# A softmax kernel whose first six loads are issued from two queues in place of one

## The chip, the core and the metric

The kernel runs on one core of one Trainium2 chip. The metric is the device time of one execution in microseconds (us), the median of several.

Four engines of the core matter. SP (SyncE) only issues transfers. ACT (ScalarE) computes the exponentials and issues the stores. DVE (VectorE) computes maxima, reciprocals and divisions. The transfers themselves are carried out by 16 DMA engines. A queue is the list in which the transfers of one issuing engine stand; in the profile SP's is q1 and ACT's is q10.

## The reference

A softmax with a temperature over the last axis of a 32 x 512 x 1024 array of float32, that is over 16,384 rows of 1024 numbers:

```
scaled = x / temperature                      # temperature 0.5
shifted = scaled - max(scaled, axis=-1)
exp_x = exp(shifted)
out = exp_x / sum(exp_x, axis=-1)
```

64 MB (67.11 million bytes) are read and as many are written, each once.

## The kernel before

The rows are cut into 16 tiles of 4 MB: 128 partitions, each with 8 whole rows (32,768 contiguous bytes). Six buffers hold tiles. A tile is loaded, worked on in place in two groups of four rows per partition, and stored; when its store is issued, the load that reuses its buffer is put into SP's queue, where it waits for that store to land.

```python
TILES = [[8]] * 16
BUFS = 6
GROUP = 4
    ...
    def load():
        i = len(tiles)
        if i < len(TILES):
            xt = data.tile([P, sum(TILES[i]), d], f32, name="xt")
            nc.sync.dma_start(out=xt, in_=dram(xf, i))          # SP's queue
            tiles.append(xt)

    def maximum(g):          # VectorE: one reduction over 128 x 4096, then the bias
        ...
    def exponential(g):      # ScalarE: 4 x exp over 128 x 1024, row sums on the way
        ...
    def divide(g):           # VectorE
        ...
        nc.vector.reciprocal(recip, sums)
        for b in range(k):
            nc.vector.tensor_scalar_mul(
                tiles[i][:, a + b, :], in0=tiles[i][:, a + b, :], scalar1=recip[:, b : b + 1]
            )

    def store(g):            # once per tile
        ...
            nc.scalar.dma_start(out=dram(of, i)[:, a : a + k, :], in_=tiles[i][:, a : a + k, :])
            ...
                load()

    with tc.manual_schedule():
        for _ in range(BUFS):
            load()
        for g in range(len(groups) + 1):
            if g < len(groups):
                maximum(g)
                exponential(g)
            if g > 0:
                divide(g - 1)
                store(g - 1)
```

## Time and profile before

| | before |
|---|---|
| time, median of 3 | 317.91 us (317.78 to 318.01) |
| bytes moved | 134.25 MB |
| VectorE busy | 235.5 us of a span of 316.0 |
| ScalarE busy | 149.6 us |
| first load landed | 12.6 us |
| VectorE starts | 13.0 us |
| last store issued | 302.4 us |

These are lines of the profile's page of the kernel before. The busy line gives microseconds and share of the span. In the DMA line each digit is the busy share of the 16 DMA engines in one fortieth of the span, in tenths, where 9 means 90% or more. The q lines give packets, MB, and the share of 16 engines' time. The next lines give the chain of waits that ended last, by engine, and the group of reductions (busy us, mean ns, then VectorE's idle time just before them and what ended it). The last two give issue to landing in us.

```profile
span 316.0 us, 620 instructions
DVE 235.5 (75%) x224; ACT 149.6 (47%) x257; POOL 0.2 (0%) x4
DMA  8999999999999999999999999999999999999996
q1 hardware_dynamic: 2304, 67.11, 49.7%
q10 hardware_dynamic: 2304, 67.11, 49.2%
q14 instruction: 4, 0.03, 0.0%
DVE 49%; DMA 32%; another core or an unknown queue 9%; ACT 5%; issue 1%; DVEq 0%; SPq 0%
L70 DVE TENSOR_REDUCE top<-xt 128x4 f32<-128x4096 f32 x32 | 141.3, 4416 | 62.6 <-DMA xt<-in_x_dram 62.6
xt<-in_x_dram SPq DMA_DIRECT2D x16, 4096.0 KB, 50.2
out_dram<-xt ACTq DMA_DIRECT2D x16, 4096.0 KB, 38.6
```

The DMA line is the one to read first: after the first slice it is 9 in every slice but the last. The two queues together hold 98.9% of the 16 engines' span. The line of the chain, which puts VectorE first with 49%, says something else and must be doubted: a chain walks back through whatever released each instruction, and it can pass through an engine whose slowness held nobody up.

The columns are from and to (us), length, busy time of VectorE, ScalarE and POOL with the number of instructions, clock, busy share of the DMA engines, and GB/s:

```profile
4.00:32.00 28.00, 18.69 (x16) 12.63 (x20) 0.00 (x0) 1.00 1.00 433
32.00:38.00 6.00, 5.93 (x6) 3.25 (x7) 0.00 (x0) 1.00 0.94 350
76.00:260.00 184.00, 140.84 (x135) 90.30 (x157) 0.00 (x0) 1.00 1.00 433
260.00:300.00 40.00, 30.03 (x30) 19.19 (x34) 0.00 (x0) 1.00 1.01 434
```

Only loads move from 4 to 32 us, loads and stores from 76 to 260. The rate is 433 GB/s in both. The one exception inside is the stretch from 32 to 38 us. The packet records of the trace show more of it than this view, because each packet of 32,768 bytes has its own start and duration there: nearly all take 1.213 us, but 16 at the start and 27 between 32 and 36 us take more, 1.3 to 2.6 us.

### The profile page before, as it was taken

The numbers are of one execution on the slowest core, as the hardware profiler recorded it, in microseconds if no ns is written. First come the engines' busy times: TensorE is split into PE (matmuls) and PEld (weight loads), VectorE is DVE, ScalarE is ACT, GpSimd is POOL, SyncE is SP. The second block draws the span as 40 slices with busy tenths as digits, with TensorE's granted clock in tenths as the row PEclk, the third lists the DMA queues.
The fourth block names the chain that finished last, engine by engine and source line by source line (L and its number), as shares of the span: only waits on it lengthen the run. The fifth ranks groups of instructions, "written<-read, shape, count | busy, mean of one in ns | idle before, by whom it ended". The sixth has DMA issues, their size and how long they took to land.

```text
span 316.0 us, 620 instructions
## 1 busy us (share of the span) xinstructions
DVE 235.5 (75%) x224; ACT 149.6 (47%) x257; POOL 0.2 (0%) x4
## 2 busy tenths in 40 slices
DVE  0399999999689494994949859497693976949720
ACT  0176666666526255361554605546064560645500
POOL 0000000000000000000000000000000000000000
DMA  8999999999999999999999999999999999999996
GB/s 332 411 452 423 373 460 415 452 425 431 436 427 440 427 444 423 444 419 448 415 452 411 452 408 456 423 444 427 436 431 432 440 423 444 419 444 419 452 411 274
DMA packets 4612, 134.25 MB, mean 425 GB/s; under 512 B 512, under 2 KB 512, under 8 KB 512
## 3 DMA queue, kind: packets, MB, share of 16 engines
q1 hardware_dynamic: 2304, 67.11, 49.7%
q10 hardware_dynamic: 2304, 67.11, 49.2%
q14 instruction: 4, 0.03, 0.0%
HBM read 67.11 MB, written 67.11 MB: 425 GB/s over the span
## 4 chain that ended last, share of the span: by engine, by line
DVE 49%; DMA 32%; another core or an unknown queue 9%; ACT 5%; issue 1%; DVEq 0%; SPq 0%
DVE top L70 29%; DMA xt<-in_x_dram 20%; DVE xt L93 18%; DMA out_dram<-xt 12%; ACT xt L79 5%; DVE recip L91 1%; DVE bias L73 1%; DVEq L147 0%; SPq L61 0%
## 5 line engine op out<-in xcount | busy, mean ns | idle before, releaser
L79 ACT ACTIVATE xt<-xt,bias 128x1024 f32<-128x1024 f32 x128 | 145.4, 1137 | 136.8 <-DVE recip L91 119.4
L70 DVE TENSOR_REDUCE top<-xt 128x4 f32<-128x4096 f32 x32 | 141.3, 4416 | 62.6 <-DMA xt<-in_x_dram 62.6
L93 DVE TENSOR_SCALAR xt<-xt,recip 128x1024 f32<-128x1024 f32 x128 | 87.7, 749 | 1.1
L79 ACT ACTIVATION_READ_ACCUMULATOR xt<-xt,bias 128x1 f32 x128 | 23.9, 187 | 0.0
L79 ACT ACT_TABLE_LOAD x1 | 1.3, 1283 | 13.0 <-DMA xt<-in_x_dram 13.0
L91 DVE RECIPROCAL recip<-sums 128x4 f32<-128x4 f32 x32 | 5.5, 171 | 2.1 <-ACT xt L79 2.1
L73 DVE TENSOR_SCALAR bias<-top 128x4 f32<-128x4 f32 x32 | 5.4, 170 | 1.1
L133 POOL MEMSET const-bfloat16-1.0<- 128x1 bf16 x1 | 0.1, 101 | 0.0
L133 POOL MEMSET const-uint8-127<- 128x1 uint8 x1 | 0.1, 101 | 0.0
L133 POOL MEMSET const-float32-0.0<- 128x1 f32 x1 | 0.1, 98 | 0.2 <-issue 0.2
L133 POOL MEMSET const-float32-1.0<- 128x1 f32 x1 | 0.1, 98 | 0.0
## 6 DMA issues: line engine op xcount, KB each, us to landing
xt<-in_x_dram SPq DMA_DIRECT2D x16, 4096.0 KB, 50.2
out_dram<-xt ACTq DMA_DIRECT2D x16, 4096.0 KB, 38.6
```

What stands on the lines that cost most here:

```text
L70: nc.vector.tensor_reduce(out=top, in_=tiles[i][:, a : a + k, :], axis=mybir.AxisListType.X, op=extreme)
L73: nc.vector.tensor_scalar_mul(bias, in0=top, scalar1=-scale)
L79: nc.scalar.activation(tiles[i][:, a + b, :], tiles[i][:, a + b, :], mybir.ActivationFunctionType.Exp, bias=bias[:, b : b + 1], scale=scal ...
L91: nc.vector.reciprocal(recip, sums)
L93: nc.vector.tensor_scalar_mul(tiles[i][:, a + b, :], in0=tiles[i][:, a + b, :], scalar1=recip[:, b : b + 1])
L133: nc = _bacc.Bacc("TRN2", target_bir_lowering=False, num_devices=1)
```

## The change

The intent is to fill the buffers sooner: ACT has nothing to do at the start, so it issues every second one of the six first loads. The later ten loads stay with SP.

```diff
         if i < len(TILES):
             xt = data.tile([P, sum(TILES[i]), d], f32, name="xt")
-            nc.sync.dma_start(out=xt, in_=dram(xf, i))
+
+            queue = nc.scalar if i < BUFS and i % 2 else nc.sync
+            queue.dma_start(out=xt, in_=dram(xf, i))
             tiles.append(xt)
```

## The prediction

> **What bounds the kernel now: the 16 DMA engines.** The page counts 134.25 MB; by the packet records of the trace 4096 packets of 32,768 bytes carry almost all of it. A packet takes 1.213 us, from either queue, in either direction: 256 per engine are 310.5 us, and 16 engines give 432 GB/s. The records have 16 packets in flight in every microsecond from 2 to 312: loads only (before 34 us), mixed, and stores only (after 282 us), all at 433 GB/s. First packet 1.74, last end 314.8. VectorE is busy 235.5 us and ScalarE 149.6 of 316.0 (page, busy times); their waits (VectorE 62.6 us for loads) are slack. The chain of waits names VectorE for 49%, which misleads: no DMA engine was starved by it.
>
> The only loss inside is slow packets: 16 at the start (one per engine, about 0.7 us over 1.213) and 22 at 34 to 37 us, just after the first store was issued on ACT's so far unused queue (median 1.66 us; about 0.8 us of bandwidth).
>
> **What the change does.** SP issues loads 0, 2, 4; ACT loads 1, 3, 5. Three issues leave SP (0.33 to 0.53 us each; all six end by 3.6 us), three of about 0.34 us come to ACT, which is idle until 13 us anyway. None is on the critical path: SP's first issue already fills the engines from 2 us on. The Trainium skill, "DMA: Bandwidth & Descriptors", section "Issuing engines are not separate DMA queues", says that DMAs of different issuers run on the same 16 engines and interleave, and that several issuers save only issuing time. This trace agrees: 433 GB/s with one queue active and with two.
>
> What moves:
> - Loads 0 and 1 share the engines packet by packet. Loads landed at 12.6, 22.3, 32.0 us; now in pairs, near 22, 41 and 61. VectorE starts near 22 instead of 13.0 us.
> - ACT's queue is first in, first out: store 0, issued near 42 us (32.7 before), stands behind load 5, starts near 60.5 and lands near 70.5 (57.1 before); load 6 is issued near 71 (57.6).
> - From 60 to 71 only stores move, then both at half rate each. The last load lands near 266 (282.1), the last store is issued near 286 (302.4); about five queued stores end the run.
>
> Engines stay full: when loads stop, stores 0 and 1 are ready. VectorE's 9 us later start is paid from its 80 us of idle time. The 310.5 us are unchanged.
>
> Only slow packets can change. If those at 34 us belong to the first use of ACT's queue, they now coincide with the start: up to 0.8 us gained. If they belong to a queue joining, they recur when SP's queue restarts near 72 us: nothing gained.
>
> **Prediction: 317.4 us** (before 317.91), eight in ten between 316.7 and 318.5. Faster by over 2%: 0.01; within 2%: 0.96; slower: 0.03.
>
> **What would show it.** Right: DMA at 9 or full in every slice, about 425 GB/s; VectorE's first wait about 22 us, the sum of its waits unchanged; longer landing of stores; last load about 16 us earlier. Wrong: fewer than 16 packets in flight near 60 to 75 us or at the end, or many packets over 1.3 us.
>
> **What would make it wrong.** A slow spell at every restart of SP's queue (ten loads, about 0.8 us each: up to 8 us slower), if that queue runs empty between loads; ACT blocked at issuing because its queue holds too much (SP's held six without blocking); uneven sharing of the engines, which would shift landings but not the sum.

## The result and the profile after

The changed kernel took 318.06 us (median of 6, 317.86 to 318.14), the kernel before 318.01 us (median of 6, 317.78 to 318.39). The ratio is 1.000, with a 95% interval from 0.9987 to 1.0012: the same. Here and below, a ratio with an interval is the mean time of one kernel's fast runs over that of the other's of the same rounds, so it is not quite the ratio of the medians that stand beside it.

The lines of the page after that answer to those above:

```profile
span 316.3 us, 619 instructions
DVE 235.1 (74%) x224; ACT 149.6 (47%) x257; POOL 0.2 (0%) x4
DMA  8999999999999999999999999999999999999995
q10 hardware_dynamic: 2736, 79.69, 58.6%
q1 hardware_dynamic: 1872, 54.53, 40.2%
q14 instruction: 5, 0.04, 0.0%
DMA 54%; DVE 32%; ACT 5%; issue 1%; DVEq 0%; SPq 0%
L72 DVE TENSOR_REDUCE top<-xt 128x4 f32<-128x4096 f32 x32 | 141.3, 4416 | 50.5 <-DMA xt<-in_x_dram 50.5
out_dram<-xt ACTq DMA_DIRECT2D x16, 4096.0 KB, 45.7
xt<-in_x_dram SPq DMA_DIRECT2D x13, 4096.0 KB, 27.0
xt<-in_x_dram ACTq DMA_DIRECT2D x3, 4096.0 KB, 41.0
```

Work moved between queues (three loads, 12.58 MB, went from q1 to q10), landing times moved, and the chain of waits now puts the DMA engines first with 54% in place of 32%. The DMA line did not move, and nor did the time. The chain's shares changed by 20 points in a kernel that takes as long as before; that is how little they say here.

In stretches:

```profile
4.00:32.00 28.00, 9.20 (x5) 6.07 (x10) 0.00 (x0) 1.00 1.00 432
32.00:38.00 6.00, 5.96 (x6) 4.38 (x8) 0.00 (x0) 1.00 1.01 437
56.00:62.00 6.00, 5.93 (x6) 3.24 (x7) 0.00 (x0) 1.00 0.97 355
76.00:260.00 184.00, 158.96 (x155) 101.76 (x175) 0.00 (x0) 1.00 1.00 432
260.00:300.00 40.00, 23.36 (x26) 14.16 (x26) 0.00 (x0) 1.00 1.01 436
```

VectorE did half as much in the first 32 us (9.20 us busy in place of 18.69), made it up later, and the DMA engines did not notice. The slow stretch is no longer at 32 to 38 us. It is at 56 to 62.

The start shows what two queues do to the first tile. These are the first steps of the chain of waits (start us, length us, what), before and then after:

```profile
0.73 12.21 DMA xt<-in_x_dram
12.96 4.43 DVE top L70
```

```profile
0.73 21.80 DMA xt<-in_x_dram
22.55 4.43 DVE top L72
```

Loads 0 and 1 take turns on the engines, packet by packet, so both land at 22.2 us; before, load 0 landed at 12.6 and load 1 at 22.3. Two queues do not bring the second tile sooner. They bring the first tile later.

The other landings, from the records of the completion marks and issues in the two traces:

| us | before | predicted | after |
|---|---|---|---|
| store 0 issued | 32.7 | 42 | 42.3 |
| store 0 landed | 57.1 | 70.5 | 71.4 |
| load 6 issued | 57.6 | 71 | 71.9 |
| last load landed | 282.1 | 266 | 269.9 |
| last store issued | 302.4 | 286 | 290.0 |
| last store landed | 314.8 | | 315.1 |
| sum of the 4096 packets' durations / 16 | 312.21 | | 312.23 |

The first packet started at 1.74 us in both. Between it and the last landing lie 313.1 us before and 313.3 after, of which 312.2 are packets on each engine. There was no idle time for the change to remove.

### The profile page after: what moved, and what is told of

Same layout as the page of the kernel before. It is cut to its first block, busy times and chain, and to the rows that moved or that the text cites. A ratio compares the mean times of both kernels' runs of the same rounds, so it can differ in the third digit from the quotient of the medians.

```text
span 316.3 us, 619 instructions
## 1 busy us (share of the span) xinstructions
DVE 235.1 (74%) x224; ACT 149.6 (47%) x257; POOL 0.2 (0%) x4
## 4 chain that ended last, share of the span: by engine, by line
DMA 54%; DVE 32%; ACT 5%; issue 1%; DVEq 0%; SPq 0%
DMA xt<-in_x_dram 41%; DVE top L72 21%; DMA out_dram<-xt 13%; DVE xt L95 10%; ACT xt L81 5%; DVE bias L75 1%; DVE recip L93 1%; DVEq L149 0%; SPq L63 0%
## 5 line engine op out<-in xcount | busy, mean ns | idle before, releaser
L72 DVE TENSOR_REDUCE top<-xt 128x4 f32<-128x4096 f32 x32 | 141.3, 4416 | 50.5 <-DMA xt<-in_x_dram 50.5
```

The lines of the kernel that those rows point to most:

```text
L72: nc.vector.tensor_reduce(out=top, in_=tiles[i][:, a : a + k, :], axis=mybir.AxisListType.X, op=extreme)
```

## The experiments

My theory: the 16 DMA engines are full in either order, so the time is the bytes; VectorE's later start is paid from slack. The rival: the change holds a gain (two queues fill faster) and an equal loss (stores stand behind loads in ACT's queue), which cancel. A second question is what makes the slow packets, on which the prediction's 0.5 us rested.

### 1. The loss alone: all six first loads on ACT's queue

```diff
-            queue = nc.scalar if i < BUFS and i % 2 else nc.sync
+            queue = nc.scalar if i < BUFS else nc.sync
```

> All six first loads from ACT's queue, so the stores stand behind loads as in the change, but the loads do not share the engines. Theory (the 16 DMA engines are full whatever the order, the rest is slack): 318.0 us, within 0.5; loads land one by one again (12.6, 22.3, 32 us), VectorE starts near 13.0 us, yet store 0, issued near 32.7, starts only after the sixth load near 60.5 and lands near 71; the seventh load is issued near 72. Rival (the change holds a gain from filling over two queues and an equal loss from stores standing behind loads): only the loss is left, several us slower than before.

Measured: 317.99 us (before in the same rounds 318.04; ratio 0.9998, 0.9982 to 1.0013). VectorE started at 13.2 us, and store 0, issued at 32.9, landed at 72.7. The DMA line of its page (the profile is of its slowest execution, 318.67 us):

```profile
DMA  8999999999999999999999999999999999999994
```

At 32.9 us three of the six loads had not landed, and the first packet of store 0 started at 61.2. So a store that stands behind three loads for 28 us costs nothing by itself. The rival's loss is not there.

### 2. The gain alone: the odd loads on POOL's queue

```diff
-            queue = nc.scalar if i < BUFS and i % 2 else nc.sync
+            queue = nc.gpsimd if i < BUFS and i % 2 else nc.sync
```

> The odd first loads from POOL's queue: loads share the engines as in the change, but no store stands behind a load. Theory: 318.0 us, within 1 (POOL's queue may have its own overhead per load, which is an unknown here); VectorE starts near 22 us, store 0 is issued near 42 and moves at once beside the loads, landing well before the 71.4 of the change. Rival (gain of filling and loss of standing behind cancel in the change): only the gain is left, several us faster than before.

Measured: 317.99 us (0.9999, 0.9985 to 1.0012). The DMA line of its page:

```profile
DMA  8999999999999999999999999999999999999996
```

The rival's gain is not there either. One part of my expectation failed: store 0, issued at 40.1 us with no load ahead of it in its queue, still landed only at 71.9. Its first packet started at 44.0, and until the last packet of SP's loads ended at 65.3 us three queues had work: of the 282 packets that started in between, 105 were the store's, 3.4 MB of its 4.19 MB. After that it still shared the engines with the last of POOL's loads, which landed at 72.8. The Trainium skill, "DMA: Bandwidth & Descriptors", section "Queues, rings and completion order", says that each engine goes round robin over the queue rows with work, a packet at a time; this landing agrees. The run therefore takes the store out of the loads' queue but does not make it land early. That the DMA time does not depend on the order is what both runs have in common.

### 3. No compute at all

```diff
             if g < len(groups):
-                maximum(g)
-                exponential(g)
+                pass
             if g > 0:
-                divide(g - 1)
                 store(g - 1)
```

> No maximum, exponential or division: each tile is stored as it was loaded (a wrong result on purpose). Theory: the time is that of the DMA traffic alone, so 317.5 to 318.2 us, with VectorE and ScalarE idle. If compute carried part of the time (the chain of waits gives VectorE 49% in the kernel before), it is clearly faster, 310 us or less. The slow packets near the first store should now lie near 13 us, where the first store is issued.

Measured: 316.70 us, with the wrong result that was intended (0.9958, 0.9945 to 0.9972). Lines of its page:

```profile
DMA  8999999999999999999999999999999999999997
q1 hardware_dynamic: 2304, 67.11, 49.9%
q10 hardware_dynamic: 2304, 67.11, 49.4%
```

All the compute of the kernel, 235.5 us of VectorE and 149.6 us of ScalarE, is worth 1.34 us of its time. This is the strongest evidence for the bound: 316.7 of 318.0 us are copying. The expectation of 317.5 at the least was missed by 0.8 us. The packets sum to 312.19 us per engine, as before. The difference is at the end: in the copy all 16 engines finish within 0.5 us (313.21 to 313.72), in the kernel before 14 of them finish by 313.82 and two at 314.42 and 314.80. The page before counts four packets on q14, instruction fetches by their kind (8 KB, 0.31 us each); the copy's page has none.

These fetches are what delays the two engines. The records do not name the engine of a packet, but a packet starts within a few nanoseconds of the end of the one before it on its engine, so that the packets can be joined into 16 chains of 256 large ones. In the kernel before, the two chains that end last hold two fetches each, and no other chain holds one. A fetch takes 0.31 us, and the packet right after it takes 1.48 to 1.75 us in place of 1.213: 1.4 us for one chain and 1.6 to 1.7 for the other. Without that both would have ended near 313.1 us, no later than the rest. In the profiles this is some 1.0 us of the 1.08 by which the last packet of the copy ends earlier; why the packet after a fetch is slow is not shown.

### 4. What makes the slow packets: a tiny store first

```diff
+    scratch = nc.dram_tensor("scratch", (P, 128), f32, kind="Internal").ap()
     with tc.manual_schedule():
+        tiny = stats.tile([P, 128], f32, name="tiny")
+        nc.vector.memset(tiny, 0.0)
+        nc.scalar.dma_start(out=scratch, in_=tiny)
```

> A 64 KB store of zeros to a scratch tensor is issued on ACT's queue at the start; all else is the kernel before. It tells what makes the slow packets at 34 to 37 us (before) and 58 to 61 us (after). If they are a single cost of the first store: they are gone at 34 to 37 us, and the time falls by up to 0.8 us, to 317.2 or so, less what the scratch store costs (about 0.2). If they are the change from loads only to stores: they are still there at 34 to 37 us, about 22 of them, and the time is 318.0 or 318.2.

Measured: 318.24 us (1.0011, 0.9998 to 1.0023), and 28 slow packets between 34 and 40 us. They are not a single cost of the first store, nor of the first use of ACT's queue. (The tiny store is 64 KB against the 4 MB of the others; that the slow packets come back before every store in runs 5 and 6 says the same.) Where they stand in the other traces, counted from the packet records (over 1.3 us, after the first 4 us; the window is the one that holds the cluster):

| kernel | first store issued, us | slow packets | window, us |
|---|---|---|---|
| before | 32.7 | 27 | 32 to 36 |
| after | 42.3, behind loads until about 61 | 22 | 56 to 60 |
| all on ACT (1) | 32.9, behind loads until about 61 | 27 | 56 to 62 |
| odd on POOL (2) | 40.1 | 29 | 42 to 46 |
| copy only (3) | 13.2 | 31 | 14 to 20 |
| early store (4) | 33.0 | 28 | 34 to 40 |

In every row the slow packets come where the first big stores begin to move, after a stretch with loads alone: all before the first packet of a store in the rows before, after and (1), some of them up to 2 us after it in (2), (3) and (4). In run 1 loads and stores share one queue, so no queue joins and none is used for the first time, and they are there all the same. What the change does is move this changeover from 35 to 59 us. Why a changeover is slow no run here shows. The few slow packets elsewhere in the kernels before and after are mostly those that follow an instruction fetch: in the traces before, after, 1, 2, 4 and 9 to 11 each of the 31 fetches inside the span is followed, 0.3 us after its start, by one packet of 1.33 to 1.78 us.

### 5 and 6. Three buffers in place of six

```diff
-BUFS = 6
+BUFS = 3
```

in the kernel before (5) and in the changed kernel (6).

> The kernel before with 3 buffers in place of 6. The engines run dry: three loads are landed at 32 us, when the first store is issued, and each later load waits for a store. A small hand model with this trace's durations (9.7 us for a load or store alone, 4.42 us for a maximum, 0.69 us per divided row) gives about 347 us, to be read against the next run.

> The changed kernel with 3 buffers. Theory (the later start of VectorE, 22.6 in place of 13.0 us, is paid from slack that six buffers give): without that slack it is paid in full, 9 to 10 us slower than the kernel before with 3 buffers. Rival (the start of VectorE doesn't matter to this kernel at all, or two queues fill faster): same or faster.

Measured: 372.97 us with one queue, 384.02 with two: 11.05 us or 3.0% slower (ratio of the medians). The lines of VectorE and of the DMA engines of the two pages, one queue and then two:

```profile
DVE 235.6 (64%) x224; ACT 149.6 (40%) x257; POOL 0.2 (0%) x4
DMA  8997899797997979979899897998979989799667
```

```profile
DVE 235.6 (62%) x224; ACT 149.6 (39%) x257; POOL 0.2 (0%) x4
DMA  8992589799798997989899898997969979798577
```

Here the engines do run dry, and the 2 and 5 in the second line are the cost: with three buffers only 12.6 MB can be loaded before the first store, and VectorE, starting at 22 us, has that store ready only at 42. By the packet records the engines stood nearly empty from 31.7 to 43.1 us, with one queue from 32.0 to 33.9: 9.4 us more. The hole cannot be filled later. The direction and size agree with the theory (9 to 10 expected; the four runs with one queue lie up to 4 us apart, so 11 is not told from 10 here). The absolute expectation of 347 us was 26 us too low: these two kernels have 588 and 590 slow packets in place of 47, and their packets sum to 331.2 and 330.7 us per engine, 19 us more than with six buffers. My model knew no slow packets. They come again and again: some 220 to 290 of each kernel stand where loads start again after a pause, like the 16 at the start of every kernel, and nearly all the others in the 5 us before the first packet of a store, where loads alone give way to stores.

### 7 and 8. Twice the maximum, so that VectorE is the bound

```diff
+        again = stats.tile([P, k], f32, name="again")
+        nc.vector.tensor_reduce(
+            out=again, in_=tiles[i][:, a : a + k, :], axis=mybir.AxisListType.X, op=extreme
+        )
         nc.vector.tensor_scalar_mul(bias, in0=top, scalar1=-scale)
```

in the kernel before (7) and in the changed kernel (8).

> The kernel before with each maximum computed twice (the second result unused), so VectorE has about 377 us of work, more than the 310.5 us of the DMA engines. About 410 us: 13.0 us to the first load, 377 us of VectorE without waits, about 20 us for the last exponential, division and store.

> The changed kernel with each maximum computed twice. Theory: where VectorE is the bound its start is on the critical path, so 9 to 10 us slower than the same with one queue (about 419.5 us). If the two are the same, the later start is hidden by something else and the theory falls.

Measured: 399.85 us with one queue and 409.70 with two, 9.85 us or 2.5% slower. The group of reductions of each, with VectorE's idle time before them at the end of the line, one queue and then two:

```profile
L70 DVE TENSOR_REDUCE top<-xt 128x4 f32<-128x4096 f32 x32 | 141.2, 4413 | 13.3 <-DMA xt<-in_x_dram 13.3
```

```profile
L72 DVE TENSOR_REDUCE top<-xt 128x4 f32<-128x4096 f32 x32 | 141.2, 4413 | 22.6 <-DMA xt<-in_x_dram 22.6
```

VectorE waits for a load once, at the start, and then never again, so the 9.3 us of later start appear whole in the time. Both times were 10 us under the expectation: VectorE's busy time was 369.8 us, not 377, which is 7 of them, and the end took about 3 us less than the 20 allowed for it.

### 9 and 10. Fewer instructions: one division per group

Run 3 suggested that fewer instructions might win back part of the 1.34 us. The four divisions of a group become one instruction, which does the same work in 4.43 us in place of 2.74 for the four:

```diff
-        for b in range(k):
-            nc.vector.tensor_scalar_mul(
-                tiles[i][:, a + b, :], in0=tiles[i][:, a + b, :], scalar1=recip[:, b : b + 1]
-            )
+        nc.vector.tensor_tensor(
+            out=tiles[i][:, a : a + k, :], in0=tiles[i][:, a : a + k, :],
+            in1=recip.unsqueeze(2).to_broadcast([P, k, d]), op=mybir.AluOpType.mult,
+        )
```

> The kernel before with the four divisions of a group as one instruction over four rows (VectorE 128 instructions in place of 224, but slower: about 4.4 us for four rows in place of 2.74, so about 289 us busy, still under 310.5). Two theories. Instruction fetches: the copy-only run had none inside its span and all 16 DMA engines ended within 0.5 us, the kernel before had four (8 KB each, on queue 14) and two engines ended over 0.6 us after the others; fewer instructions should mean fewer fetches and up to 1.3 us less. Compute at the end: after the last load, landed at 282 us, about 3 us more VectorE work stand before the last store, which was issued at 302.4 us when 2.7 us of stores were still queued; so the queue now runs empty for 1 to 3 us. Together 317.5 to 320 us.

> The changed kernel with the same merged division. Its last store is issued near 290 us with some 15 us of stores still queued, so the longer VectorE work at the end stays hidden: 316.8 to 317.9 us if fewer instruction fetches help, 318.0 if they don't, and 0.5 to 2 us faster than the same with one queue. If it is equal to the run with one queue, the earlier last load of the change is worth nothing even here.

Measured: 318.12 us with one queue (0.9996, 0.9984 to 1.0009), as expected, and 327.21 us with two (1.0283, 1.0269 to 1.0297). I had expected the changed kernel to be the faster of the two; it is 9.1 us slower. Lines of the pages, one queue and then two:

```profile
DVE 288.4 (91%) x128; ACT 149.5 (47%) x257; POOL 0.2 (0%) x4
DMA  8999999999999999999999999999999999999987
L70 DVE TENSOR_REDUCE top<-xt 128x4 f32<-128x4096 f32 x32 | 141.2, 4411 | 13.1 <-DMA xt<-in_x_dram 13.1
```

```profile
DVE 288.4 (89%) x128; ACT 149.5 (46%) x257; POOL 0.2 (0%) x4
DMA  7999999999999999999999999999999999991947
L72 DVE TENSOR_REDUCE top<-xt 128x4 f32<-128x4096 f32 x32 | 141.2, 4411 | 22.5 <-DMA xt<-in_x_dram 22.5
```

And the end of the second in stretches (the last two columns are the DMA engines' busy share and GB/s):

```profile
296.00:300.00 4.00, 4.00 (x2) 3.71 (x8) 0.00 (x0) 1.00 0.00 0
300.00:310.00 10.00, 9.73 (x6) 4.64 (x8) 0.00 (x0) 1.00 0.98 419
310.00:314.00 4.00, 3.45 (x1) 0.00 (x0) 0.00 (x0) 1.00 0.00 0
```

My mistake was to count from the last load, which does land earlier in the changed kernel (269.4 us, 277.9 with one queue). VectorE had no time to wait for it. It starts once, works 288.4 us, and so ends no earlier than 13.1 + 288.4 = 301.5 or 22.5 + 288.4 = 310.9 us; the last stores were issued at 304.1 and 313.5. To keep the DMA engines full to the end the last store must be there when the store before it ends, at about 305 us. One start still reaches that, nearly: the engines of run 9 stood idle from about 303.5 to 305. The other does not. VectorE's 91% with one queue was a kernel at the edge, and the 9 us of the later start push it over, while the DMA line still shows 9 almost everywhere.

### 11. A version that beats both

One queue, and the merged division for all but the last six groups, so that VectorE catches up before the end:

```diff
+        if g < len(groups) - 6:
+            nc.vector.tensor_tensor(
+                ...   # as in runs 9 and 10
+            )
+            return
         for b in range(k):
             nc.vector.tensor_scalar_mul(
```

> One queue, merged division as in the merged runs but for the last six groups (tiles 13 to 15), which divide row by row as before, in 2.74 us. With everything merged the DMA engines stood idle from about 303.5 to 305 us because the last store was issued at 304.1; here it should be issued near 300 us, while the store before it is still moving, so no hole. With fewer instruction fetches as well: 316.7 to 317.3 us, 0.2 to 0.4% under both kernels and close to the 316.70 of copying alone. If it is 318.0, fewer fetches are worth nothing and the copy-only run owed its lead to something else.

Measured: 317.25 us (before 317.94; ratio 0.9979, 0.9965 to 0.9992). The last store was issued at 298.0 us, the engines stayed full, and the last landing came at 314.16 in place of 314.80. It is 0.2% faster than the kernel before, a small but clear gain, and 0.55 us above copying alone, which was run in other rounds on another chip. The changed kernel was not in these rounds; that this version beats it too rests on the changed kernel being no faster than the one before. The gain fits the fetches (three in place of four inside the span): in the chains of packets the engine that ends last again carries fetches, which cost it 1.1 us here and 1.6 to 1.7 in the kernel before, and it ends 0.64 us earlier. No run separates this from all else that the edit changes.

## Why the prediction was right, and which of its steps were not

- **The bound, and "the 310.5 us are unchanged": right.** Copying alone takes 316.70 us (run 3), and the packets sum to 312.2 us per engine before and after. The skill's section "Issuing engines are not separate DMA queues", on which this rested, agrees with runs 1 and 2: three further ways to place the first loads, 317.99 to 318.06 us.
- **"Loads 0 and 1 share the engines packet by packet": right.** They landed at 22.2 us, the pairs after them at 41.5 and 61.8 (near 41 and 61 predicted).
- **"VectorE's 9 us later start is paid from its 80 us of idle time": right, and tested.** Where that slack is taken away the 9 us appear: 9.85 us in runs 7 and 8, 9.1 us in runs 9 and 10. The step is incomplete, though, as runs 5 and 6 show: there VectorE is idle for 135 and 147 us, longer than before, and the later start still costs 11.05 us. Idle time of VectorE pays only while the DMA engines have other work; six loads, which last until 62 us, gave them that, and three did not.
- **"The last load lands near 266, the last store is issued near 286": right in direction, 4 us off in size.** The mis-sized term is the time that load 6 needs to get going: issued at 71.9 us, its first packet started at 75.8, so 3.9 us, while I had let it share the engines at once. All later loads follow it.
- **"The sum of VectorE's waits unchanged": wrong.** The waits for loads fell from 62.6 to 50.5 us. VectorE is idle for as long as before (316.0 less 235.5, 316.3 less 235.1), but it now finishes 12.4 us earlier (its last division ends as the last store is issued, 290.0 in place of 302.4), and idle time after an engine's last instruction is in no wait.
- **"If those at 34 us belong to the first use of ACT's queue ... If they belong to a queue joining": both wrong.** I named two causes for the slow packets, and the trace after showed a third place: 22 of them at 56 to 60 us, ahead of the first stores, and none when SP's queue starts again (load 6 starts at 75.8; the only two nearby, at 73.8 and 73.9, each follow an instruction fetch, as two at 65.3 did before). They belong to the changeover from loads alone to loads and stores (run 4 and its table), and every order of this kernel has one. So the 0.5 us that the prediction allowed for them was not gained, which is most of the distance from 317.4 to 318.06.

Between two runs of the same kind the scatter is about 0.1%, so the case cannot show whether the change costs or gains 0.2 us. Nothing in the packets suggests either.

## What to carry to other kernels

Here, where the DMA engines were busy in every slice, a second queue did not fill buffers faster: it only divided the same 433 GB/s among more transfers, so the first tile came later and the second no sooner. Whether that hurts is asked of the engine that waits for the first tile: add its start, its busy time and its tail, and compare with the time when the DMA engines need the last store; here 23 + 235 us was harmless and 23 + 288 us cost 9. Also make sure that the DMA engines have loads queued until it has caught up; with three buffers they had not. Shares of a chain of waits changed here by about 20 points while the time stood still, so look for the resource that is never idle before believing them.

## What the Trainium skill lacked or had wrong

- "DMA: Bandwidth & Descriptors", section "Issuing engines are not separate DMA queues": right (runs 1 and 2), but it lacks the price. Splitting the first loads over two queues delayed the first tile from 12.6 to 22.2 us, which cost 9.1 to 11.05 us in the three pairs of kernels that could not hide it.
- The same page, section "Where 436 GB/s comes from": it says that the HBM side, about 358 GB/s, binds transfers between HBM and SBUF. The section lacks the condition that the page gives under its table of one core (425 GB/s at 16 MB): that a core gets about 358 GB/s when both cores of a pair stream. This core, alone, moved 433 GB/s with loads only, with both directions, and with stores only, which is close to the 435 GB/s that the section gives for the fabric.
- The same page, section "Specifications", gives about 0.6 us to the first byte for the path of SP and ACT, without saying from where it counts. Here the first packet started 1.0 us after the start of the first issue (0.73 to 1.74 us) and 0.64 us after its end (1.10), which agrees; but it started 4.5 us (store 0 before, 32.7 to 37.1) and 3.9 us (load 6 after) after an issue on an empty queue while the engines were busy with another. The page has no figure for that case.
- No page that I read has the slow changeover: 22 to 31 packets of 1.3 to 2.6 us in place of 1.213 each time loads alone give way to loads with stores, 0.8 to 1.0 us once per run here. In the kernels with three buffers these and the slow first packets after a pause come to some 19 us per engine.
- No page that I read says what instruction fetches cost a kernel that is bound by DMA; "Runtime: NRT & Kernel Launch", section "Instruction fetch mechanics", where it belongs, has no figure for it. Here a fetch took 0.31 us of one engine, and the packet after it 0.1 to 0.6 us more than 1.213. Two on the same engine delayed the end of the kernel before by about 1.0 us.
